# Softmax over rows: the last four loads move from SyncE's queue to ScalarE's

## The chip, the cores and the metric

The kernel runs on one core of a Trainium2 chip. The metric is the device time of one execution in microseconds (us); lower is better.

## The reference

The input is float32 of shape 16 x 1024 x 512. Each row of 512 numbers is halved and goes through a softmax:

```python
x_scaled = x / 2.0
x_max = np.max(x_scaled, axis=-1, keepdims=True)
exp_x = np.exp(x_scaled - x_max)
out = exp_x / np.sum(exp_x, axis=-1, keepdims=True)
```

Input and output are 33.55 MB each, and every byte is read once and written once.

## The kernel before

The 16384 rows are spread over 128 partitions, which makes 128 rows of 512 numbers on each partition. They are cut into 12 tiles, t0 to t11, of 3, 7, 15, 15, 15, 15, 15, 15, 15, 7, 3 and 3 rows a partition (the list `PLAN`, lines 11 to 14). A tile is one load and one store: 768 KB for 3 rows, 1792 KB for 7, 3840 KB for 15. In this text L8 is the load of tile t8 and S8 its store.

All tiles lie in one buffer in on-chip memory, `arena`, which has room for 100 rows a partition. Tiles t0 to t7 fill it. The last four tiles take the place of earlier ones: t8 lies where t2 was, t9 where t1 was, t10 where t0 was and t11 on part of t3. The dictionary `behind` (lines 65 to 70) finds this out, so a load of t8 to t11 may only be issued once the store of the earlier tile has landed.

The work on a tile is cut into chunks of 3 to 5 rows a partition, 28 in all (c0 to c27); a 15-row tile is three chunks of 5. For each chunk there are three steps:

- VectorE takes the maximum of each row (`do_max`, line 89), after the tile's load has landed.
- ScalarE takes the exponential and sums it up, one instruction for each row of the partition (line 122).
- VectorE takes the reciprocal of the sums (line 98) and multiplies (line 102 in tiles t1 to t3, line 109 in the others).

VectorE's order is written out by hand with `LAG = 2`: the maximum of chunk k, then the multiplication of chunk k - 2. So the multiplication of c25, which ends tile t9, stands behind the maximum of c27, which needs tile t11. The chunks that end tiles t4, t6, t8, t9, t10 and t11 are c11, c17, c23, c25, c26 and c27.

The queues: ScalarE issues L0 to L7 at the start, before its first exponential (line 85). SyncE issues everything else, in the order S0 S1 S2 S3 S4 L8 L9 L10 S5 L11 S6 S7 S8 S9 S10 S11. Each store waits there for the last multiplication of its tile (line 144). L8 to L11 wait for the landing of the store whose place they take (line 151). Work that one engine issues shares one queue, and a queue's transfers are carried out in the order of issue.

Of the kernel before, what the change touches and what calls it, by code (L numbers as in the profile page):

```python
# [1 line left out]

# [4 lines left out]

PLAN = [  # L11
    ([3], 0), ([4, 3], 3), ([5] * 3, 10), ([5] * 3, 25), ([5] * 3, 40), ([5] * 3, 55),
    ([5] * 3, 70), ([5] * 3, 85), ([5] * 3, 10), ([4, 3], 3), ([3], 0), ([3], 25),
]
ARENA = 100
LAG = 2

FUSED = {1, 2, 3}


@with_exitstack
def kernel(
    ctx: ExitStack,
    tc: tile.TileContext,
    x: bass.AP,
    out: bass.AP,
):
    nc = tc.nc
    fp32 = mybir.dt.float32

    xf = x.flatten_outer_dims()
    of = out.flatten_outer_dims()
    N, D = xf.shape
    P = nc.NUM_PARTITIONS
    n_rows = N // P
    assert sum(sum(c) for c, _ in PLAN) == n_rows

    arena = nc.alloc_sbuf_tensor("arena", (P, ARENA, D), fp32)
    negmax = nc.alloc_sbuf_tensor("negmax", (P, n_rows), fp32)
    sums = nc.alloc_sbuf_tensor("sums", (P, n_rows), fp32)  # L40
    recip = nc.alloc_sbuf_tensor("recip", (P, n_rows), fp32)

    tiles, chunks, base = [], [], 0
    for t, (cs, at) in enumerate(PLAN):
        r = sum(cs)
        tiles.append((base, r, at))
        o = 0
        for c in cs:  # L50
            chunks.append((t, base + o, c, at + o))
            o += c
        base += r
    last_chunk = {c[0]: k for k, c in enumerate(chunks)}

    def dram(ap, t):
        b, r, _ = tiles[t]
        return ap[b * P : (b + r) * P].rearrange("(p r) d -> p r d", r=r)

    def sb(t):  # L60
        _, r, at = tiles[t]
        return arena[:, at : at + r, :]


    behind = {}
    for t, (_, r, at) in enumerate(tiles):
        for u in range(t):
            _, ru, au = tiles[u]
            if at < au + ru and au < at + r:
                behind.setdefault(t, []).append(u)  # L70

    ld = [tc.alloc_semaphore(f"ld{t}") for t in range(len(tiles))]
    awaited = sorted({u for us in behind.values() for u in us})
    st = {t: tc.alloc_semaphore(f"st{t}") for t in awaited}
    s_end = tc.alloc_semaphore("s_end")
    s_max = tc.alloc_semaphore("s_max")
    s_exp = tc.alloc_semaphore("s_exp")
    s_rec = tc.alloc_semaphore("s_rec")
    s_mul = tc.alloc_semaphore("s_mul")

    def issue_loads(begin, end):

        for t in range(begin, end):
            if t not in behind:
                nc.scalar.dma_start(out=sb(t), in_=dram(xf, t)).then_inc(ld[t], 16)

    def do_max(k):
        t, b, c, a = chunks[k]
        nc.vector.reduce_max(  # L89
            out=negmax[:, b : b + c],  # L90
            in_=arena[:, a : a + c],
            axis=mybir.AxisListType.X,
            negate=True,
        )._wait_ge(ld[t], 16).then_inc(s_max, 1)

    def do_mul(k):
        t, b, c, a = chunks[k]
        nc.vector.reciprocal(  # L98
            out=recip[:, b : b + c], in_=sums[:, b : b + c]
        )._wait_ge(s_exp, k + 1).then_inc(s_rec, 1)  # L100
        if t in FUSED:
            nc.vector.tensor_mul(  # L102
                out=arena[:, a : a + c],
                in0=arena[:, a : a + c],
                in1=recip[:, b : b + c].unsqueeze(2).to_broadcast([P, c, D]),
            )._wait_ge(s_rec, k + 1).then_inc(s_mul, 1)
            return
        for r in range(c):
            ins = nc.vector.tensor_scalar_mul(  # L109
                out=arena[:, a + r],  # L110
                in0=arena[:, a + r],
                scalar1=recip[:, b + r : b + r + 1],
            )
            if r == 0:
                ins._wait_ge(s_rec, k + 1)
        ins.then_inc(s_mul, 1)

    def compute_and_store():

        for k, (t, b, c, a) in enumerate(chunks):  # L120
            for r in range(c):
                ins = nc.scalar.activation(  # L122
                    out=arena[:, a + r],
                    in_=arena[:, a + r],
                    func=mybir.ActivationFunctionType.Exp,
                    bias=negmax[:, b + r : b + r + 1],
                    scale=0.5,
                    accum_out=sums[:, b + r : b + r + 1],
                )
                if r == 0:  # L130
                    ins._wait_ge(s_max, k + 1)
            ins.then_inc(s_exp, 1)


        for k in range(len(chunks) + LAG):
            if k < len(chunks):
                do_max(k)
            if k >= LAG:
                do_mul(k - LAG)


        late = sorted(behind)
        for t in range(len(tiles)):
            nc.sync.wait_ge(s_mul, last_chunk[t] + 1)
            nc.sync.dma_start(out=dram(of, t), in_=sb(t)).then_inc(
                st[t] if t in awaited else s_end, 16
            )
            while late and max(behind[late[0]]) <= t - 2:
                u = late.pop(0)
                for v in behind[u]:  # L150
                    nc.sync.wait_ge(st[v], 16)
                nc.sync.dma_start(out=sb(u), in_=dram(xf, u)).then_inc(ld[u], 16)

        for t in awaited:
            nc.gpsimd.wait_ge(st[t], 16)
        nc.gpsimd.wait_ge(s_end, 16 * (len(tiles) - len(awaited)))

    hook = nc.inst_callbacks[-1]  # L160
    nc.remove_inst_callback(hook)
    symbolic = nc._always_lower_symbolic_ap
    nc._always_lower_symbolic_ap = False
    here = str(nc.cur_bb)
    entry = nc.main_func.blocks[0]
    head, jumps = entry.instructions[:-5], entry.instructions[-5:]
    entry.instructions = []
    nc.switch_bb("main", None)
    issue_loads(0, 2)
    first = list(entry.instructions)  # L170
    at = next(k for k, i in enumerate(head) if type(i).__name__ == "InstDrain")
    entry.instructions = head[:at] + first + head[at:]
    issue_loads(2, len(tiles))
    compute_and_store()
    entry.instructions = list(entry.instructions) + jumps
    nc.switch_bb(here, None)
    nc._always_lower_symbolic_ap = symbolic
    nc.push_inst_callback(hook)


# [1 line left out]
_INS = ['x']  # L182
_OUTS = [((16, 1024, 512), 'float32')]


# [23 lines left out]
```

## Time and profile before

| | |
|---|---|
| median of 5 runs | 162.61 us (162.4 to 163.71) |
| the profiled execution's own time | 162.61 us |
| its span, first to last instruction | 160.8 us |
| VectorE busy | 131.7 us, 82% of the span |
| ScalarE busy | 94.5 us, 59% |
| DMA traffic | 67.13 MB, mean 417 GB/s over the span |
| queue q10 (what ScalarE issues) | 26.21 MB |
| queue q1 (what SyncE issues) | 40.90 MB |

The span leaves out 1.8 us of the profiled execution's time. In the profile DVE is VectorE, ACT is ScalarE, SP is SyncE, and ACTq and SPq are the DMA queues that these two issue into. A share of the DMA engines is a mean over the core's 16; 1.00 means that all of them moved data all of the time. A packet is one contiguous piece that one of these engines moves: 30 KB for a 15-row tile, 14 KB for 7 rows, 6 KB for 3 rows.

### The profile page before, as it was taken

To read this page: it belongs to the slowest core of one execution; us is meant where nothing else is said; L and a number is where in the kernel's file an instruction comes from. 1 tells how busy PE (TensorE), PEld (TensorE's weight loads), DVE (VectorE), ACT (ScalarE), POOL (GpSimd) and SP (SyncE) were. 2 spreads that over 40 slices of the span, in tenths; PEclk is the share of its full clock that TensorE was granted. 3 is DMA by queue.
4 is the path that set the end of the run, shared out by engine and by line. 5 is a ranking of instruction groups with operands and counts; after the bars stand their busy time and mean duration, and the time that the engine had idled before them with its cause. 6 is when DMAs were issued, how large, how long until landed. Compare 5 with 4: busy or idle time off the path is not lost.

```text
span 160.8 us, 480 instructions
## 1 busy us (share of the span) xinstructions
DVE 131.7 (82%) x155; ACT 94.5 (59%) x257; POOL 0.2 (0%) x4
## 2 busy tenths in 40 slices
DVE  0475599999999999999999999999999999970000
ACT  0739076759547746866669766688666875620000
POOL 0000000000000000000000000000000000000000
DMA  7999999999998999999999999999999999999993
GB/s 251 481 409 466 413 439 410 351 461 385 480 413 382 474 397 458 443 413 453 405 474 390 474 390 460 397 425 435 457 405 440 436 420 466 397 466 397 423 402 160
DMA packets 3459, 67.13 MB, mean 417 GB/s; under 512 B 384, under 2 KB 384, under 8 KB 1152
## 3 DMA queue, kind: packets, MB, share of 16 engines
q1 hardware_dynamic: 2304, 40.90, 59.3%
q10 hardware_dynamic: 1152, 26.21, 38.8%
q14 instruction: 3, 0.02, 0.0%
HBM read 33.55 MB, written 33.55 MB: 417 GB/s over the span
## 4 chain that ended last, share of the span: by engine, by line
DVE 77%; DMA 10%; issue 0%; DVEq 0%
DVE negmax L89 40%; DVE arena L109 22%; DVE arena L102 13%; DMA arena<-in_x_dram 10%; DVE recip L98 2%; DVEq L204 0%
## 5 line engine op out<-in xcount | busy, mean ns | idle before, releaser
L122 ACT ACTIVATE arena<-arena,negmax 128x512 f32<-128x512 f32 x128 | 90.7, 710 | 42.7 <-DVE negmax L89 42.7
L89 DVE TENSOR_REDUCE negmax<-arena 128x5 f32<-128x2560 f32 (+2 forms) x28 | 72.3, 2585 | 11.0 <-DMA arena<-in_x_dram 11.0
L109 DVE TENSOR_SCALAR arena<-arena,recip 128x512 f32<-128x512 f32 x91 | 37.8, 482 | 0.7
L122 ACT ACTIVATION_READ_ACCUMULATOR arena<-arena,negmax 128x1 f32 x128 | 23.9, 187 | 0.0
L102 DVE TENSOR_TENSOR arena<-arena,recip 128x2560 f32<-128x2560 f32 (+2 forms) x8 | 21.0, 2625 | 0.3
L98 DVE RECIPROCAL recip<-sums 128x5 f32<-128x5 f32 (+2 forms) x28 | 4.9, 176 | 0.0
L122 ACT ACT_TABLE_LOAD x1 | 1.3, 1283 | 4.5 <-issue 4.5
L193 POOL MEMSET const-bfloat16-1.0<- 128x1 bf16 x1 | 0.1, 102 | 0.0
L193 POOL MEMSET const-uint8-127<- 128x1 uint8 x1 | 0.1, 102 | 0.0
L193 POOL MEMSET const-float32-1.0<- 128x1 f32 x1 | 0.1, 99 | 0.0
L193 POOL MEMSET const-float32-0.0<- 128x1 f32 x1 | 0.1, 98 | 0.2 <-issue 0.2
## 6 DMA issues: line engine op xcount, KB each, us to landing
out_dram<-arena SPq DMA_DIRECT2D x7, 3840.0 KB, 21.6
arena<-in_x_dram ACTq DMA_DIRECT2D x6, 3840.0 KB, 47.0
arena<-in_x_dram SPq DMA_DIRECT2D x1, 3840.0 KB, 29.8
out_dram<-arena SPq DMA_DIRECT2D x2, 1792.0 KB, 16.6
out_dram<-arena SPq DMA_DIRECT2D x3, 768.0 KB, 15.6
arena<-in_x_dram ACTq DMA_DIRECT2D x1, 1792.0 KB, 8.4
arena<-in_x_dram SPq DMA_DIRECT2D x1, 1792.0 KB, 33.5
arena<-in_x_dram SPq DMA_DIRECT2D x2, 768.0 KB, 33.9
```

The source lines that it names most:

```text
L89: nc.vector.reduce_max(out=negmax[:, b : b + c], in_=arena[:, a : a + c], axis=mybir.AxisListType.X, negate=True,)._wait_ge(ld[t], 16).the ...
L98: nc.vector.reciprocal(out=recip[:, b : b + c], in_=sums[:, b : b + c])._wait_ge(s_exp, k + 1).then_inc(s_rec, 1)
L102: nc.vector.tensor_mul(out=arena[:, a : a + c], in0=arena[:, a : a + c], in1=recip[:, b : b + c].unsqueeze(2).to_broadcast([P, c, D]),)._w ...
L109: ins = nc.vector.tensor_scalar_mul(out=arena[:, a + r], in0=arena[:, a + r], scalar1=recip[:, b + r : b + r + 1],)
L122: ins = nc.scalar.activation(out=arena[:, a + r], in_=arena[:, a + r], func=mybir.ActivationFunctionType.Exp, bias=negmax[:, b + r : b + r ...
L193: nc = _bacc.Bacc("TRN2", target_bir_lowering=False, num_devices=1)
```

## The change

L8, L9, L10 and L11 are no longer issued by SyncE. ScalarE issues them, between its exponentials: L8, L9 and L10 before the first exponential of tile t5 (chunk c12), and L11 before the first exponential of tile t7 (chunk c18). Each still waits for the store whose place it takes, now on ScalarE. SyncE issues the twelve stores and nothing else.

```diff
+AFTER = {8: 4, 9: 4, 10: 4, 11: 6}
...
+        late = sorted(behind)
         for k, (t, b, c, a) in enumerate(chunks):
+            while late and last_chunk[AFTER[late[0]]] < k:
+                u = late.pop(0)
+                for v in behind[u]:
+                    nc.scalar.wait_ge(st[v], 16)
+                nc.scalar.dma_start(out=sb(u), in_=dram(xf, u)).then_inc(ld[u], 16)
             for r in range(c):
                 ins = nc.scalar.activation(
...
-        late = sorted(behind)
         for t in range(len(tiles)):
             nc.sync.wait_ge(s_mul, last_chunk[t] + 1)
             nc.sync.dma_start(out=dram(of, t), in_=sb(t)).then_inc(
                 st[t] if t in awaited else s_end, 16
             )
-            while late and max(behind[late[0]]) <= t - 2:
-                u = late.pop(0)
-                for v in behind[u]:
-                    nc.sync.wait_ge(st[v], 16)
-                nc.sync.dma_start(out=sb(u), in_=dram(xf, u)).then_inc(ld[u], 16)
```

## The prediction

> **What bounds the kernel now.** I read the page's slices and queues first, then a table of stretches, then single queues in short windows, and last the rows of single transfers. All times are microseconds from the start of the span.
>
> ```profile
> DMA  7999999999998999999999999999999999999993
> q1 hardware_dynamic: 2304, 40.90, 59.3%
> q10 hardware_dynamic: 1152, 26.21, 38.8%
> DVE 77%; DMA 10%; issue 0%; DVEq 0%
> ```
>
> The DMA engines are busy in every slice, and the two queues take 59.3% + 38.8% = 98% of 16 engines over the span. The chain of waits (last line) says 77% VectorE, but only because it follows the last instruction back through VectorE, and VectorE is done early. The table of stretches shows it (columns: stretch, its length, busy time of VectorE, ScalarE and GpSimd with counts, clock, DMA share, GB/s):
>
> ```profile
> 18.00:93.00 75.00, 74.42 (x67) 50.82 (x140) 0.00 (x0) 1.00 1.00 428
> 93.00:113.00 20.00, 19.86 (x29) 14.64 (x41) 0.00 (x0) 1.00 1.00 428
> 113.00:143.70 30.70, 30.37 (x54) 20.53 (x56) 0.00 (x0) 1.00 1.02 437
> 143.70:150.00 6.30, 0.00 (x0) 0.00 (x0) 0.00 (x0) 1.00 0.94 405
> 150.00:158.00 8.00, 0.00 (x0) 0.00 (x0) 0.00 (x0) 1.00 0.98 417
> 158.00:160.80 2.80, 0.00 (x0) 0.00 (x0) 0.00 (x0) 1.00 0.12 48
> ```
>
> VectorE ends at 143.7, and the DMA engines then work 16 us more on stores that were ready and queued. Up to 158 they hardly rest. So the bytes and the rate of the DMA engines set the end, and VectorE has a reserve. The change moves the same bytes. It can move the end only if it leaves the DMA engines without work, or changes their rate. The rate looks the same with loads beside stores (428 GB/s up to 93) and with stores alone (437 and 417 later), so I count nothing for a rate.
>
> **How two queues share.** Window 18.2 to 27.9 holds S0 (6 KB packets, q1) beside L3 (30 KB packets, q10); columns are packets, MB, share:
>
> ```profile
> q10 hardware_dynamic: 112, 3.44, 83.1%
> q1 hardware_dynamic: 116, 0.71, 17.5%
> ```
>
> The engines alternate packet by packet (112 to 116), not byte by byte (3.44 to 0.71 MB). A queue of small packets gets a small share beside one of large packets. In window 98 to 105 a single queue moves 98 packets of 30 KB:
>
> ```profile
> q1 hardware_dynamic: 98, 3.01, 99.8%
> ```
>
> That is 16 x 7.0 x 0.998 / 98 = 1.14 us a packet on one engine; by size, 0.53 for 14 KB and 0.23 for 6 KB. A transfer gives each of 16 engines 128 / 16 = 8 packets. Alone, a 15-row transfer takes 9.1 us, a 7-row one 4.3, a 3-row one 1.9.
>
> **The change part by part.** Up to 68 nothing differs.
>
> *Four issues and their waits on ScalarE.* Around c12 the timeline of ScalarE reads:
>
> ```profile
> 68.25 0.19 ACT L122 ACTIVATION_READ_ACCUMULATOR arena<-arena,negmax 128x1 f32 x1
> 69.73 0.72 ACT L122 ACTIVATE arena<-arena,negmax 128x512 f32<-128x512 f32 x1 [1.29 <-DVE negmax L89]
> ```
>
> S2, for which L8 waits, was issued at 45.0 and landed 21.6 later, at 66.6, before ScalarE gets there; S0 and S1 landed long before. The three issues cost about 0.5 each (the loads on ScalarE's queue took 335 to 669 ns) = 1.5, of which 1.29 fits the idle time. The 0.2 left delays c12's exponentials. Queued behind them are ScalarE's later chunks, and VectorE's multiplication of c12, which begins at 79.6, over 5 us after these exponentials end at 73.4: no cost. If S2 landed 3 us later, that would still be covered. L11's issue before c18 fits an idle time of 1.29 too, and S3 (issued 62.1, waiting at most until L11's old issue at 92.0) is in by then.
>
> *SyncE loses four issues.* They took 0.5 to 0.7 each in a queue that mostly waited for VectorE: nothing.
>
> *The loads stand behind L7 in ScalarE's queue, beside the stores.* This is the part that counts. Before, L8 to L10 followed S4 in one queue and ran alone from 98 to 113, while S5 waited. Now stores and loads alternate. The rows of the last three early loads give the pace:
>
> ```profile
> L85 ACTq DMA_DIRECT2D arena<-in_x_dram x3: 466/500/501, 3.0 to 4.0; - x3
> DMA to landing us min/median/max: 54.1/71.7/89.4
> ```
>
> L5, L6 and L7 land at 57.1, 75.2 and 93.4, so 18.2 for each load of 15 rows beside 30 KB stores: 9.1 of its own and 9.1 of the stores' turns. Store work is there all the time (S4 to S8 are ready when needed: S5 at 91.6, S6 at 106.4, S7 at 121.2, S8 at 134.4). So L8 lands at 93.4 + 18.2 = 111.6, L9 at + 4.3 + 9.1 = 125.0, L10 at + 1.9 + 9.1 = 136.0 and L11 at + 11.0 = 147.0. Before, L8 landed at 77.2 + 29.8 = 107.0 and L11 at 92.0 + 32.5 = 124.5. One packet more or less is 1.1 us.
>
> *What waits for them.* VectorE wanted t8 at 111.3, t9 at 126.1, t10 at 134.4 and t11 at 137.8. L8 is 0.3 late, L9 early, L10 1.6 late, L11 9.2 late. Behind the maximum of c27 stand on VectorE:
>
> ```profile
> 137.75 1.75 DVE L89 TENSOR_REDUCE negmax<-arena 128x3 f32<-128x1536 f32 x1
> 139.41 0.17 DVE L98 RECIPROCAL recip<-sums 128x3 f32<-128x3 f32 x1
> 139.61 1.28 DVE L109 TENSOR_SCALAR arena<-arena,recip 128x512 f32<-128x512 f32 x3
> ```
>
> and SyncE's queue holds the stores that these release (its last row, S8 to S11; S9 is issued at 140.9):
>
> ```profile
> 134.40 9.64 SPq L145 DMA_DIRECT2D out_dram<-arena  x4
> ```
>
> The multiplication at 139.6 is c25's, which releases S9 at 140.9. Now 147.0 + 3.1 (137.8 to 140.9) = 150.1. S10 and S11 follow at 151.5 and 152.9, and VectorE ends at 152.9 instead of 143.7.
>
> *Whether the DMA engines run dry.* All loads and S0 to S8 are the same bytes as before, so S8 ends where it ended: it landed at 134.4 + 17.4 = 151.8 on the last engine, and on the first about 1.4 earlier (the engines end between 158.0 and 159.4 too). S9 is issued at 150.1. From issue to packets I have two rows. On an empty queue, the first load was issued at 0.13, had no packet by 1.1 and 14 by 1.4, so 1.0 to 1.3. On busy engines S0, issued at 14.35, had none by 18.1, so 3.8. S9 comes to a queue that is just running out, nearest to the first row: packets from 151.1 to 151.6. The engines that ended S8 first idle for about 1 us, the last ones for 0 to 0.2. S9, S10 and S11 take 4.3 + 1.9 + 1.9 = 8.0, as before (S11 landed at 143.7 + 16.0 = 159.7, 7.9 after S8). The late engines end as before, the early ones 0 to 0.5 later than the late ones: 151.6 + 8.0 + 0.3 to land = 159.9 against 159.7 (in the window 158 to 160 the last packet ends at 159.4, and S11 landed 0.3 later). A start from empty adds something: the first load took 4.6 to land where its data are 1.9, so 2.7 at most, and 150.1 + 2.7 + 8.0 = 160.8, which is +1.1. With 3.8 to the first packet it is 150.1 + 3.8 + 8.0 + 0.3 = 162.2, +2.5. Below, nothing: 0 if L11 is one packet earlier. I take +0.6, between +0.2 and +1.1, since some engines are still busy and some empty. Span 161.4; with the 1.8 outside it 163.2. The profiled run's time is the median, 162.61.
>
> Two sentences from the Trainium skill, which the sum doesn't need. The page "DMA: Bandwidth & Descriptors", section "Issuing engines are not separate DMA queues", says that transfers from several issuers interleave on the same 16 engines and that a second issuer saves only issue time; by it alone the change is worth nothing, 162.6, but it leaves out who goes first, which the 112 to 116 packets show. The same page, section "Specifications", gives about 0.6 us to the first byte on these queues; the first load's row has 1.0 to 1.3, and by 0.6 the sum would be 162.8.
>
> **Rivals.** A difference under 0.5%, 0.8 us, is about what a measurement of this kernel can't tell from none: 161.8 to 163.4 is "same".
>
> - *Slower: S9 comes after the store queue is empty by more than a short gap.* Place: VectorE, c25's multiplication behind c27's maximum behind L11. Price: 1 us for each us that S9 is issued after about 150.3, so it decides over 0.8 from there, and up to the 3.8 row. One store packet more for each of the four loads is 4 x 1.14 = 4.6 later (167.8); one more in all gives 164.3. For it: 6 KB loads have the smallest share, and the engines' spread adds to the landing, which needs the last engine. Against: the alternation was one to one to within 4%. Chance 0.40.
> - *No gap at all.* L11 lands by 146, S9 is in the queue before S8 ends: 162.6. For it: only one packet is needed. It is also the case in which the new order means nothing. Chance 0.12.
> - *Faster.* The engines end between 158.0 and 159.4; if the pause evened them out, 0.7 could be gained at the most, and a little on noise: 161.7. No bytes or rate change otherwise. Chance 0.04.
>
> **The numbers.** My forecast, a short gap, has 0.44 at 163.2; its own range is 162.6 to 163.4. With "no gap" that makes 0.56 for the same, 0.40 slower, 0.04 faster. The range: low 162.3 leaves out the faster case and a little below no gap; high 164.8 takes in most of the slower case (+2.2), and leaves out about 0.12 above.
>
> **What would show it.** Right: L8 to L11 landing near 112, 125, 136 and 147; VectorE ending near 153 instead of 143.7, with a wait of about 9 us on a load at line 89 and little else new; S9 issued near 150; a dent in the DMA share between 150 and 152; ScalarE without a wait for a store. Wrong: loads that land early (a share by bytes), a DMA rate off 428 to 437 GB/s where both directions run, or S9 issued long after S8 has landed.

## The result and the profile after

The changed kernel takes 162.22 us (median, 161.77 to 162.79) against 162.64 us for the kernel before (162.04 to 163.71): ratio 0.9971, 95% interval 0.9964 to 0.9979. It is 0.4 us faster: small, but the interval leaves out 1. I had forecast 163.2, with 162.3 as the low end of the range. The result lies in the band that I had called the same (161.8 to 163.4), but on the other side of the kernel before, and just below the range; "faster" in my sense, by over 0.5%, it is not. The profiled execution after has a span of 160.3, before 160.8.

From the page of the changed kernel:

```profile
q10 hardware_dynamic: 1728, 33.56, 49.6%
q1 hardware_dynamic: 1728, 33.56, 48.8%
DVE 49%; DMA 38%; another core or an unknown queue 5%; ACT 2%; issue 0%; DVEq 0%
```

All loads are now on q10 and all stores on q1, 33.56 MB each. The chain of waits shows a lot of DMA (38% instead of 10%), since VectorE waits for the late loads; the time didn't follow it. The last two stretches (length, VectorE, ScalarE, GpSimd, clock, DMA share, GB/s):

```profile
150.00:158.00 8.00, 2.50 (x7) 0.60 (x2) 0.00 (x0) 1.00 0.93 389
158.00:160.30 2.30, 0.00 (x0) 0.00 (x0) 0.00 (x0) 1.00 0.32 128
```

VectorE works beyond 150 (before, it had stopped at 143.7), the DMA share dips to 0.93 in the stretch from 150, and in the last stretch the engines are busier (0.32 instead of 0.12). VectorE's timeline after, around t10 and t11 (start, duration, operation, and in brackets the idle time ahead and who ended it; rows between these are left out):

```profile
135.65 1.75 DVE L91 TENSOR_REDUCE negmax<-arena 128x3 f32<-128x1536 f32 x1 [1.13 <-DMA arena<-in_x_dram]
146.59 1.75 DVE L91 TENSOR_REDUCE negmax<-arena 128x3 f32<-128x1536 f32 x1 [7.39 <-DMA arena<-in_x_dram]
148.46 1.28 DVE L111 TENSOR_SCALAR arena<-arena,recip 128x512 f32<-128x512 f32 x3
```

and SyncE's last stores, with the landing rows of the four late loads (issued at 67.2, 67.6, 68.1 and 94.4):

```profile
149.76 3.13 SPq L152 DMA_DIRECT2D out_dram<-arena  x3
```

```profile
L128 ACTq DMA_DIRECT2D arena<-in_x_dram x4: 335/404/481, 67.2 to 94.4; - x4
DMA to landing us min/median/max: 44.2/54.7/67.5
```

L8 lands at 67.2 + 44.2 = 111.4, L10 at 68.1 + 67.5 = 135.6, and by their own rows L9 at 67.6 + 57.1 = 124.7 and L11 at 94.4 + 52.2 = 146.6. c27's maximum starts at 146.6, and S9 is issued at 149.8. All this stands in the prediction within 0.4 us (111.6, 125.0, 136.0, 147.0, 150.1). Then a part of the DMA engines rests, as forecast. The window from 149.5 to 151.5 in 40 slices of 0.05 us; such a row counts a packet whole in the slice where it starts, and the last 30 KB packets of S8 run on for 1.14 us:

```profile
DMA  0090990000000000000006999060600099960606
```

The engine that ends S8 first is through at 150.2 and has nothing until S9 brings packets at slice 22, 150.55. So the mechanism came as described, and yet the time fell. What differs is when the *last* engine is through. The tail of both kernels, window 157.5 to 161.5 in 40 slices of 0.1 us, first before and then after:

```profile
DMA  9497864324041110200000000000000000000000
```

```profile
DMA  9989298997920000000000000000000000000000
```

Before, the engines drop out one by one from 158.0 to 159.4; after, all end by 158.9 (the last packets start in the slices from 159.1 and 158.6 and take 0.23). My first theory read the cause off this: the short rest lets all engines start S9 together ("E", evening out). It is wrong, as the runs show. The number that counts stands earlier, in the landing row of S8. First before, then after:

```profile
L145 SPq DMA_DIRECT2D out_dram<-arena x1: 332/332/332, 134.4 to 134.4; - x1
DMA to landing us min/median/max: 17.4/17.4/17.4
```

```profile
L152 SPq DMA_DIRECT2D out_dram<-arena x1: 332/332/332, 134.5 to 134.5; - x1
DMA to landing us min/median/max: 16.8/16.8/16.8
```

S8 has landed on all engines at 134.5 + 16.8 = 151.3; before, at 134.4 + 17.4 = 151.8. From there to the landing of S11 (159.2 and 159.7) it is 7.9 us in both. Between these two executions the 0.5 us were won before S9 and its rest.

### The profile page after: what moved, and what is told of

It reads as the page before. It is cut to its first block, busy times and chain, and to the rows that moved or that the text cites. A ratio compares the mean times of both kernels' runs of the same rounds, so it can differ in the third digit from the quotient of the medians.

```text
span 160.3 us, 480 instructions
## 1 busy us (share of the span) xinstructions
DVE 132.0 (82%) x155; ACT 94.5 (59%) x257; POOL 0.2 (0%) x4
## 3 DMA queue, kind: packets, MB, share of 16 engines
q10 hardware_dynamic: 1728, 33.56, 49.6%
q1 hardware_dynamic: 1728, 33.56, 48.8%
## 4 chain that ended last, share of the span: by engine, by line
DVE 49%; DMA 38%; another core or an unknown queue 5%; ACT 2%; issue 0%; DVEq 0%
DMA arena<-in_x_dram 38%; DVE negmax L91 25%; DVE arena L104 13%; DVE arena L111 10%; ACT arena L130 2%; DVE recip L100 1%; DVEq L206 0%
## 6 DMA issues: line engine op xcount, KB each, us to landing
arena<-in_x_dram ACTq DMA_DIRECT2D x7, 3840.0 KB, 44.2
arena<-in_x_dram ACTq DMA_DIRECT2D x3, 768.0 KB, 52.2
```

## The experiments

Each ratio is to the kernel before on the same chip, with its 95% interval. Of the orders I write the queue of SyncE only; what is not in it is on ScalarE. The kernel before is S4 L8 L9 L10 S5 L11 S6 and so on.

**Is it the rest before S9?** Three runs. The first takes the rest away, by moving two multiplications ahead of the wait for t11:

```diff
         for k in range(len(chunks) + LAG):
+            if k == len(chunks) - 1:
+                do_mul(k - 2)
+                do_mul(k - 1)
             if k < len(chunks):
                 do_max(k)
-            if k >= LAG:
+            if k >= LAG and not len(chunks) - 3 <= k - LAG <= len(chunks) - 2:
                 do_mul(k - LAG)
```

> The changed kernel, with VectorE's multiplications of c25 and c26 put ahead of the maximum of c27, so that S9 and S10 are issued about 8 to 10 us sooner (near 140 and 142) and the store queue never runs out before S9. Theory E (the short rest of the DMA engines before S9 let early and late engines start S9 together, and that evening out is the gain): the gain goes, 162.6, and the last packets spread over 1.4 us again. Theory M (the gain was made before S9: the small loads of t9 to t11 now run beside 30 KB stores, where their slow first packets no longer hold up the engines that are late): the gain stays, 162.2 or a little less, S8 lands near 151.3 and S11 near 159.2.

Measured: 162.30, ratio 0.9977 (0.9963 to 0.9991). S9 was issued at 140.6, no rest is left, and the gain stays.

The second puts the rest into the kernel before:

```diff
+            if k == len(chunks) - 1:
+                for i, n in enumerate([5, 5, 5, 1]):
+                    nc.vector.reduce_max(out=spare[:, 5 * i : 5 * i + n], in_=arena[:, 85 : 85 + n], ...)
             if k >= LAG:
                 do_mul(k - LAG)
```

> The kernel before, with four row maxima more on VectorE (16 rows, about 8.8 us, written to a spare buffer) between the maximum of c27 and the multiplication of c25, so that S9 is issued near 149.8 as in the changed kernel and the DMA engines rest before it, while all loads stay where they were. Theory E: 162.2, S11 landing within 0.3 us on all engines. Theory M: no gain, 162.6 to 162.9, since the late engines come no sooner.

Measured: 162.69, ratio 1.0002 (0.9986 to 1.0018). S9 was issued at 149.7 and a part of the engines rested, and there is no gain. Theory E falls from both sides. A second profile of the changed kernel, taken in a later run, says the same: there L11 landed 1.0 us sooner, S9 was issued at 148.8, before the first engine had ended S8 (150.3), and the engines ended S11 1.0 us apart; the time was 162.08, against 162.09 in the first profile with its rest.

The third makes the rest longer in the changed kernel (output as before; S9 only waits):

```diff
             nc.sync.wait_ge(s_mul, last_chunk[t] + 1)
+            if t == 9:
+                nc.sync.wait_ge(s_end, 80)
```

> The changed kernel, with S9 held on SyncE until all engines have landed S8 (near 151.3), so it is issued 1.6 us later than in the changed kernel. My prediction's price of 1 us for each us of rest on the last engine: first packets near 152.3 instead of 150.7 to 150.9, 163.5 to 163.7. If the store queue had work of another kind to cover this, or a rest costs nothing: 162.2.

Measured: 163.71, ratio 1.0059 (1.0038 to 1.0080). Window 149.5 to 152.5 of this run, 40 slices of 0.075 us:

```profile
DMA  0990000000000000000000000000000000999000
```

S9, issued at 151.25, has its first packets at slice 35, 152.05: 0.8 us after the issue, as in the changed kernel (149.76 to 150.55). S11 lands 1.5 us later than there, for an S9 issued 1.5 us later. The price of 1 us for 1 us holds once the rest reaches the last engine. The rest in the first profile of the changed kernel was just short enough not to cost anything. The Trainium skill, page "DMA: Bandwidth & Descriptors", section "Latency and other measured facts", gives about 600 ns to the first byte on these queues; these two rows have 0.8.

**Is it the small loads?** Theory M: load packets of 6 and 14 KB that run alone are slow on some engines. Half of the change each:

```diff
-        late = sorted(behind)
+        late = [9, 10, 11]
...
+            if t == 4:
+                nc.sync.wait_ge(st[2], 16)
+                nc.sync.dma_start(out=sb(8), in_=dram(xf, 8)).then_inc(ld[8], 16)
```

> L9, L10 and L11 are issued by ScalarE as in the changed kernel, L8 stays on SyncE's queue behind S4. The small loads then run from 93 beside S4 and L8 and land before VectorE needs them, so there is no rest before S9. Theory E: 162.6. Theory M: 162.2.

Measured: 162.33, ratio 0.9988 (0.9970 to 1.0007): not told apart from no change, though the median is that of theory M.

The other half, with `late = [8]` and SyncE's order S4 L9 L10 S5 L11 S6:

> The other half of the change: only L8 is issued by ScalarE; L9, L10 and L11 stay on SyncE behind S4 and S5. L9 runs in part beside L8, L10 and L11 run alone. Theory M: most of the gain is missing, 162.5 to 162.7. If it is L8 beside the stores that brings the gain: 162.2.

Measured: 162.14, ratio 0.9965 (0.9948 to 0.9981): the whole gain, with the small loads where they were. Theory M expected the opposite.

**Does the order in SyncE's queue matter?** All loads as before on SyncE, only the order changes:

```diff
-            while late and max(behind[late[0]]) <= t - 2:
-                u = late.pop(0)
-                for v in behind[u]:
-                    nc.sync.wait_ge(st[v], 16)
+            for u in {4: [8, 9], 5: [10], 6: [11]}.get(t, []):
+                nc.sync.wait_ge(st[behind[u][0]], 16)
```

> All late loads on SyncE as before, in the order S4 L8 L9 S5 L10 S6 L11 S7: L10 no longer follows L9 and L8 in a stretch of loads alone but stands behind a store. Theory M in its narrow form (the slow packets of L10 at 111 to 112, 0.32 to 0.69 us instead of 0.23, came from small loads right behind other loads): 162.2. Theory E, and a theory M in which any small load that runs alone is slow: 162.6.

Measured: 163.59, ratio 1.0071 (1.0049 to 1.0093). Nobody expected that: 0.9 us slower, from the place of two small loads that no one waits for. Its tail (157.5 to 161.5) and its S8:

```profile
DMA  9494361514041141101111110110100000000000
```

```profile
L144 SPq DMA_DIRECT2D out_dram<-arena x1: 343/343/343, 134.3 to 134.3; - x1
DMA to landing us min/median/max: 18.6/18.6/18.6
```

The first engines are out at 158 as ever, the last go on to 160.6; S8 lands at 153.0 (134.35 + 18.64). Next, every late load alone between two stores, `{4: [8], 5: [9], 6: [10], 7: [11]}`:

> All late loads on SyncE, each alone between two stores: S4 L8 S5 L9 S6 L10 S7 L11 S8. L11 lands near 144 instead of 124.5, about 6 us after VectorE wants it, but S9 is still issued near 147, before S8 ends. Theory M (6 and 14 KB load packets that run alone are slow on some DMA engines, and an engine that falls behind stays behind to the end): three small loads behind stores, as slow as the order with two of them or slower, 163.6 to 164.5. Theory T (each turn of a single queue from stores to loads and back costs the late engines, whatever the packets' size): four turns instead of three, 164.0 to 164.5. Theory N (the order of the single queue does not matter, the last slower run had another cause): 162.6.

Measured: 163.61, ratio 1.0056 (1.0034 to 1.0078). The queue goes from loads back to stores four times here, three times in the order with L10 behind S5 and twice in the kernel before. I call that a turn. Four turns are no slower than three; theory T had 164.0 at the least.

Then three turns again, without small packets in the late loads. The plan's last 28 rows are cut anew, `([4, 4], 10), ([5, 5], 25), ([5, 5], 0)`, and the order is `{4: [8], 5: [9], 6: [10]}`:

> The last 28 rows in three tiles of 8, 10 and 10 rows (packets of 16 and 20 KB) instead of 15, 7, 3 and 3, all late loads on SyncE in the order S4 L8 S5 L9 S6 L10 S7: three turns to loads, as in the slower order with L10 behind S5 and L11 behind S6, but no small load packets after the start. Theory M: no slow packets, 162.2 to 162.6. Theory T: 163.6.

Measured: 163.28, ratio 1.0026 (1.0006 to 1.0045), between the two. Packets of 20 KB are hit as well, so M in its first form falls. I looked for the slow packets in the trace of each run: load packets on SyncE's queue that took over 60 ns more than their usual 0.234, 0.535, 0.61, 0.76 or 1.14 us. Most of them are among the *last* packets of a load behind which a store stands in the same queue: of 83 such packets of 6 to 20 KB in late loads, over ten profiles, 79 start in the second half of their load's 128 packets and 62 in the last quarter. In the run with four turns L9 was hit in its middle as well. In the run with L10 behind S5 these were L9's last packets (up to 0.90 instead of 0.535), L10's (up to 0.82 instead of 0.234) and L11's (up to 1.09). L9 had none in the two profiles of the kernel before, where L10 follows it, and seven here, where S5 follows. That is theory B: the queue loses time where it turns back from loads to stores. A slow load packet alone is no sign of a turn, though: ScalarE's queue, by the same measure, has 60 to 102 of them in the first 60 us of every profile, the changed kernel's too. After 100 us it has none.

**Fewer turns.** All loads on SyncE in one stretch, `{4: [8, 9, 10, 11]}`:

> All late loads on SyncE in one stretch, S4 L8 L9 L10 L11 S5: the single queue turns back from loads to stores once instead of twice, and the last load packets before that turn are of 6 KB. Theory B (the last engine loses time where a single queue turns back from loads to stores while the other queue is empty: the last load packets there are slow, up to 0.7 to 1.6 us, on a few engines): one turn costs about half of before's loss, 162.2 to 162.5. Theory M (small load packets that run alone are slow, wherever they stand): the same three small loads alone, 162.6 or more.

Measured: 162.27, ratio 0.9974 (0.9956 to 0.9992). This has the gain of the change with no load moved to ScalarE at all. With the 30 KB load ahead of the turn, `{4: [9, 10, 11, 8]}`:

> As the order with one turn, but L9 L10 L11 L8: the packets ahead of the turn are of 30 KB. L8 lands near 115, some 3.5 us after VectorE wants it, which its reserve covers. Theory B with any packet size: 162.2 to 162.5. Theory B with small packets only, and theory M if the small packets at the turn are the cause: 162.2. If small load packets alone are slow anywhere: 162.6.

Measured: 162.38, ratio 0.9985 (0.9968 to 1.0002): no slow packet ahead of the turn, but no better time. One turn of each of the two in the kernel before, the first (`late = [11]` on ScalarE, `{4: [8, 9, 10]}` on SyncE) and the second (`late = [8, 9, 10]`, `{5: [11]}`):

> Only L11 moves to ScalarE; SyncE keeps S4 L8 L9 L10 S5 and so turns back from loads to stores once, behind L10. Theory B, with the loss of the kernel before shared by its two turns or growing with their number: 162.2 to 162.5. If the turn behind L10 alone makes the loss (its slow packets were seen there in the trace of before): 162.6.

> L8, L9 and L10 on ScalarE as in the change, L11 on SyncE behind S5: the only turn back is that behind L11, with L8 to L10 running beside it. Theory B: a turn costs where the other queue is empty, so none, 162.2. If L11's turn costs wherever it stands: 162.4 to 162.7.

Measured: 162.23, ratio 0.9982 (0.9965 to 0.9999), and 162.48, ratio 0.9993 (0.9980 to 1.0006). The first has a gain, just clear of noise; the second can't be told from the kernel before, where theory B expected 162.2. The intervals don't tell the two apart, so what each turn is worth stays open.

**L8 on ScalarE with three turns**, `late = [8]`, `{4: [9], 5: [10], 6: [11]}`:

> L8 on ScalarE as in the run that had the whole gain with it, and the others on SyncE one by one between stores: S4 L9 S5 L10 S6 L11 S7, three turns back, two of them after L8 has ended. Theory B: those turns cost as in the slow orders, 163.0 to 163.6. If L8 beside the stores protects all that comes later: 162.1 to 162.3.

Measured: 162.54, ratio 0.9995 (0.9972 to 1.0018). That is far less than the 0.9 us of three turns without it, and neither of the two expected results. The median is 0.4 us over that of the order with L8 on ScalarE and two turns, but the intervals overlap, so a cost of these turns isn't shown. There is something in L8 beside the stores that theory B doesn't hold.

**The kernel before, a second profile:**

> The kernel before once more, for a second profile of the same order. Theory B: slow load packets again stand only ahead of the two turns, and the time follows how late the last engine ends S8: landing of S8 plus 7.9 us for S9 to S11.

Measured: one time, 163.03, span 161.2. Slow packets again, three of L10's last (0.32 to 0.42) and four of L11's last (0.32 to 0.90), both ahead of a turn. Its S8:

```profile
L145 SPq DMA_DIRECT2D out_dram<-arena x1: 332/332/332, 134.4 to 134.4; - x1
DMA to landing us min/median/max: 17.8/17.8/17.8
```

It lands at 152.2, 0.4 later than in the first profile of the same kernel, and the profiled time is 0.42 longer. So the same kernel has a different loss from execution to execution.

**Both cures together**, `late = [8]` on ScalarE, `{4: [9, 10, 11]}` on SyncE, and once more beside the changed kernel on the same chip:

> L8 on ScalarE and L9 L10 L11 in one stretch on SyncE behind S4. If L8 beside the stores brings a gain of its own, beside that of fewer turns: 161.8 to 162.0. If both only take away the same late packets, and the rest of the span is bytes: 162.2.

> L8 on ScalarE, L9 L10 L11 in one stretch on SyncE behind S4, once more beside the changed kernel on the same chip. If the late packets behind the turns are the whole difference and this order has the fewest: 161.9 with a narrow spread of times, 0.3 us below the changed kernel, whose rest before S9 also starts some engines late.

> The changed kernel on the same chip: 162.2 by its earlier median, with S11 landing within 0.3 us on all engines and 7.9 us after S8. If the order with L8 alone on ScalarE is no better: the two within 0.1 us of each other.

Measured: 161.87 (161.85 to 161.92 in 5 runs), ratio 0.9958 (0.9943 to 0.9972), and again 161.94 (161.82 to 162.16 in 9), ratio 0.9959 (0.9941 to 0.9978). Beside it the changed kernel had 162.28 (162.08 to 162.66 in 12), ratio 0.9982 (0.9968 to 0.9997). This version beats the changed kernel and the one before on the same chip, by about 0.3 and 0.6 us. The changed kernel's engines landed S11 1.0 us apart here, not within 0.3. Its tail:

```profile
DMA  7934443140000000000000000000000000000000
```

**A longer first load** in the changed kernel, `([3, 4, 3], 0)` for the first two tiles:

> The changed kernel with the first two tiles (3 and 7 rows) joined to one of 10 rows, so that the first load has packets of 20 KB; VectorE starts about 4 us later and has that reserve. The engines end the first load 0.9 us apart in the changed kernel; if that spread comes from the small first packets and lasts to the end, 161.7 to 162.0; if not, 162.2, and 162.5 if the later first store costs something.

Measured: 162.43, ratio 0.9991 (0.9972 to 1.0011). No gain; the spread of the engines does not come from the small first packets alone. Its profile, without any turn, has the store of the last 15-row tile (S8 in the other orders) at 150.1 on the first engine and at 151.9 on the last.

**The profiles side by side** (orders with the plan of before). A store signals its end once for each of the 16 engines. The first and last of these signals for S8, from the traces, with the slow load packets after 100 us on SyncE's queue ("both cures" is the second of its two runs):

| kernel | turns on SyncE | slow packets | S8 on the first engine | on the last | profiled time |
|---|---|---|---|---|---|
| both cures | 1 | 0 | 150.1 | 151.0 | 161.8 |
| L8 on ScalarE | 2 | 0 | 150.2 | 151.2 | 162.0 |
| L11 alone on SyncE | 1 | 1 | 150.2 | 151.2 | 162.0 |
| changed kernel | 0 | 0 | 150.2 | 151.3 | 162.1 |
| changed kernel again | 0 | 0 | 150.3 | 151.3 | 162.1 |
| small loads on ScalarE | 1 | 0 | 150.4 | 151.4 | 162.2 |
| one turn, 30 KB load last | 1 | 0 | 150.2 | 151.5 | 162.2 |
| before, with a rest | 2 | 4 | 150.3 | 151.5 | 162.3 |
| changed, no rest | 0 | 0 | 150.3 | 151.5 | 162.3 |
| one turn | 1 | 5 | 150.2 | 151.5 | 162.3 |
| L11 on ScalarE | 1 | 1 | 150.2 | 151.8 | 162.6 |
| before | 2 | 10 | 150.4 | 151.8 | 162.6 |
| L8 on ScalarE, three turns | 3 | 3 | 150.0 | 151.8 | 162.6 |
| before again | 2 | 7 | 150.1 | 152.2 | 163.0 |
| four turns | 4 | 25 | 150.3 | 152.6 | 163.4 |
| L10 behind S5 | 3 | 17 | 150.2 | 153.0 | 163.8 |

The first engine ends S8 at the same time in all, to 0.4 us: the bytes haven't changed. The profiled time is the last engine's S8 plus 10.8 us in every row; only the run with the longer rest, which is left out, has more (12.4). So the difference between these kernels is how late the last engine is, and nearly all of that is how far it has fallen behind the first.

The same signals for the transfers ahead of S8 show where it falls behind. In the order with L10 behind S5 the last engine is 1.0 us behind the first at S4, 1.5 at L9 and S5, 2.2 at L10 and S6, 2.7 at L11 and 2.8 at S7 and S8: the gap grows at the loads ahead of a turn and keeps in between. In the kernel before it goes from 0.6 at S4 to 1.4 at S8, in its second profile from 1.0 to 2.1, with the largest step, 1.4 to 2.0, at L11. In the changed kernel it goes from 1.3 to 1.1, in its second profile from 1.2 to 1.0. But not every gap comes from a turn: with L8 on ScalarE and three turns it was 1.7 at S4 already, before the first of these turns, and 1.8 at S8. And the count of slow packets doesn't give its size: with L11 on ScalarE there was one slow packet, and S8 ended on the last engine when it did in the kernel before, which had ten.

## Why the prediction was wrong

- **What bounds the kernel** was right, as far as it went: bytes and rate of the DMA engines, not VectorE, which ended 9 us later for nothing. But I took the 16 engines as one. No engine takes over another's work (in the order with L10 behind S5 the first had nothing more from 158, while others went on to 160.6), and the end is that of the last. The share of 1.00 in the stretches can't show that.
- **The packet-by-packet alternation** and the landings worked out from it were right to 0.4 us, and so were S9's issue (150.1, measured 149.8) and the rest. The second profile, with S9 at 148.8 and no rest, shows that such a match has some luck in it.
- **ScalarE's four issues** cost nothing, as I said, though not for the reason I gave. ScalarE's timeline after:

```profile
67.18 0.34 ACTq L128 DMA_DIRECT2D arena<-in_x_dram  x1
67.49 0.19 ACT L130 ACTIVATION_READ_ACCUMULATOR arena<-arena,negmax 128x1 f32 x1
67.56 0.47 ACTq L128 DMA_DIRECT2D arena<-in_x_dram  x1
67.58 0.71 ACT L130 ACTIVATE arena<-arena,negmax 128x512 f32<-128x512 f32 x1
...
69.68 0.72 ACT L130 ACTIVATE arena<-arena,negmax 128x512 f32<-128x512 f32 x1 [1.29 <-DVE negmax L91]
```

  The queue goes ahead of the engine: the issues are made while the exponentials of c11 still run, and the idle time before c12 is 1.29 as before.
- **The step that failed** is "All loads and S0 to S8 are the same bytes as before, so S8 ends where it ended: it landed at 134.4 + 17.4 = 151.8 on the last engine". It landed at 151.3. The bytes are the same, but the last engine's delay isn't: the gap between the first and the last engine, which grows from S4 to S8 in the kernel before, doesn't in the changed one. I had seen the 1.4 us between the first and last engine and used them only as slack for the rest. I never asked what made them, and whether a load moved to the other queue would take that away. Removing four loads from SyncE was costed at "nothing", by the issue time alone; that their places in the queue behind and ahead of stores had a price was not in the sum.
- **A term mis-sized:** from S9's issue to its packets I took 1.0 to 1.3 and added up to 1.1 for a start from empty. It took 0.8, and no addition is seen on the last engine (7.9 us from S8's to S11's landing, as before). With these, and S8 as before, the sum would have given 162.6, "no gap". With S8 at 151.3 it gives 162.1.
- **The rivals.** "Faster" had the size about right (up to 0.7; it was 0.4) and the wrong mechanism: a rest that evens out the engines is worth nothing, as the run with a rest in the kernel before shows. "Slower" had the right price, shown by the longer rest. Its point was nearer than I put it: S11 lands 9.5 after S9's issue in the first profile of the changed kernel and in the run with the longer rest, and 149.8 + 9.5 = 159.2 is just where the last engine ends too (151.3 + 7.9). By these numbers each us from 149.8 on, not from 150.3, would have cost one.
- **The Trainium skill's rule** on issuers (page "DMA: Bandwidth & Descriptors", section "Issuing engines are not separate DMA queues": all issuers' transfers interleave on the same 16 engines, a second issuer saves only issue time) would have given 162.6. It is nearer than my forecast, but the runs don't bear it out: the same loads with another division and order on the two queues span 161.9 to 163.6. Issue time is no part of that: S8 and S9 were issued at 134.3 and 140.9 in the slowest order with three turns, and at 134.4 and 140.9 in the kernel before.

What is shown: the time follows the last engine's end of S8; the rest before S9 is not the cause; with all late loads on SyncE, slow load packets stand ahead of the turns back to stores (none in the order with the 30 KB load last), the last engine falls behind there, and three or four turns are slower than two; one turn, with no load moved to ScalarE, brings about as much as the change. What stays open: what makes the packets ahead of a turn slow, what opens the gap of 0.6 to 1.7 us that is there before the first turn, and why two turns with L8 on ScalarE had no slow packet and cost nothing, where the same two turns had 10 and 7 in the two profiles of before. That counting turns alone gives the time is refuted by that run.

## What to carry to other kernels

When the DMA engines are the bound, look at the last of them, not at the mean: compare the end of the tail and the landing of the last large transfers, since the gap that opened at a turn here lasted to the end. Where loads share a queue with stores, try them in one stretch or on the other queue; one by one between stores they cost 0.9 us here. A rest before the last transfers cost nothing until it reached the engine that was last, and then 1 us for 1 us; the cheapest trial here was the order in the queue.

## What the runs showed of the hardware

- The place of two 768 KB loads in a queue, which nothing waited for, was worth 0.9 us (163.59 against 162.69).
- Load packets just ahead of a store in the same queue took up to 0.9 us in the kernel before (usual: 0.23) and up to 1.09 in the slowest order, and in different numbers in two executions of the same kernel (10 and 7).
- The spread of a kernel's times shrank with the spread of its engines: 161.82 to 162.16 with both cures (9 runs), 162.0 to 163.4 for the kernel before on the same chip (20 runs).
